# First adaLN part of a DiT layer kernel: k tiles in four column blocks of the TensorE array

## The chip, the cores and the metric

One core of a Trainium2 chip runs the whole layer in one launch. The metric is the device time of one execution in microseconds (us). The engines are named as in the profile: PE is TensorE (PEld its weight loads), DVE is VectorE, ACT is ScalarE, POOL is GpSimd, and SP issues the DMAs. Every engine takes its instructions strictly in the order of its own queue, and waits at the head of the queue until the semaphores of that instruction are there.

## The reference, cut to what matters

The layer works on 1024 latent tokens and 256 context tokens, both 1024 wide. The part that is changed is the adaLN modulation of the first normalisation:

```python
sh1, sc1, g1, sh2, sc2, g2 = ada_split(c, w_ada, b_ada)          # latents
csh1, csc1, ...            = ada_split(c_ctx, w_ada, b_ada)      # context
# ada_split: jnp.split(jax.nn.silu(cond) @ w_ada + b_ada, 6)
h   = LN(x)   * (1 + sc1)  + sh1
h_c = LN(ctx) * (1 + csc1) + csh1
p   = h @ W_in
```

So two vectors of 1024 values (SiLU of c and of c_ctx) are multiplied by the first 2048 columns of w_ada, 8 MB of float32. All of it is float32, and the kernel keeps that accuracy.

## The kernel before

The program begins with the first adaLN part, `ada1`. It runs over eight column groups j = 0 to 7. Group j gives shift and scale of 128 channels, that is 256 columns of w_ada, and its weights come in two DMAs of 512 KB (`wa{j}_0` with k tiles 0 to 3, `wa{j}_1` with k tiles 4 to 7) into a pool of seven buffers (`x_tile`, tag "x"), which the two context tiles `x_c0` and `x_c1` and later the latent tiles share. A DMA into a buffer waits until the last reader of what was in it is done, and no more than eight DMAs are under way, since their eight semaphores are used in turn.

`ada1_mm(j)` (L264) multiplies. The stationary operand is the pair of SiLU vectors for one k tile, padded with zeros to 128 columns; the moving operand is 128x256 of the weights. Five k tiles (L270) are plain float32 matmuls, each of which the profile shows as two MATMUL passes. The last three k tiles (ADA_SPLIT) go through `mm3` (L206 to L209): the weights are split into a rounded part `ahi` (ACT, L121) and the rest `alo` (DVE, L122), and three single-pass matmuls are made of them. All eight add up in one PSUM tile `pa_{j}`, of which two rows count. DVE copies these out as `arow_{j}` (L276).

`ada1_fin(j)` (L279) turns the two rows into columns with two small transposes (L282) into `pat_{j}`, and DVE adds the bias (L284, `mod`).

Between these stands the work on the context: statistics of the two context tiles (L178, L180), the POOL power (L171), the normalised tile `z_c0`, `z_c1` (L250), its transposes on PE (L188), shift and scale on ACT (L298, `hc`), and the split into `Hhi` (ACT, L305) and `Hlo` (DVE, L306), first for channels 0 to 511, after j = 3, and then for the rest. The 256 context tokens then go through the k columns of W_in (`kctx`, weights `hi_K`, `lo_K`), then both contexts and the eight latent chunks through the v and gate columns (`vg_8_0`, `vg_8_1`, `vg_9_0`, ... , weights `hi_VG`, `lo_VG`), with each latent chunk's own normalisation and split (`Hhi` L197, `Hlo` L198) in between, and the q weights (`hi_Q`, `lo_Q`) prepared beside them.

The kernel is written in a Tile framework that places the instructions of each engine in an order of its own, with a model of the times, when the program is built; that order is then fixed. Which instruction stands behind which on each engine is therefore not the order of the source lines.

Of the kernel before, what the change touches and what calls it, by code (L numbers as in the profile page):

```python
# [10 lines left out]
F32 = mybir.dt.float32  # L11
F32R = mybir.dt.float32r
AF = mybir.ActivationFunctionType
ALU = mybir.AluOpType
# [3 lines left out]
P = 128  # L18
# [4 lines left out]
KT = 8  # L23
# [7 lines left out]
BATCHES = (4, 3, 3, 3, 3)  # L31
USLOTS = (9, 29)
SLOT = 2112
ADA_SPLIT = 3


@with_exitstack
def layer_kernel(ctx: ExitStack, tc: tile.TileContext, I: dict, out: bass.AP, dbg=None):
    nc = tc.nc
    V, S, G, T = nc.vector, nc.scalar, nc.gpsimd, nc.tensor  # L40

    def dma(o, i):
        nc.sync.dma_start(o, i)
# [11 lines left out]
    wpool = wst.enter_context(tc.tile_pool(name="wpool", bufs=4))  # L55
# [19 lines left out]
    def ps_nm(name):  # L75
        return ps_next("nm", 5, 3, name)
# [19 lines left out]
    econ = early.enter_context(tc.tile_pool(name="econ", bufs=1))  # L96
# [3 lines left out]
    sp = st0.enter_context(tc.tile_pool(name="start", bufs=2, reuse_waits="tile"))  # L100

    def x_tile(name):
        return sp.tile([P, D], F32, tag="x", bufs=7, name=name)
# [4 lines left out]
    ada_w = []  # L108

    def ada1_load(j):  # L110
        rw = [x_tile(f"wa{j}_{i}") for i in range(2)]
        for i in range(2):
            dma(rw[i], I["wada1"][j, :, i * D : (i + 1) * D])
        hi = wpool.tile([P, SLOT], F32R, tag="whi", name=f"ahi_{j}").rearrange("p (k c) -> p k c", c=264)
        lo = wpool.tile([P, SLOT], F32R, tag="wlo", name=f"alo_{j}").rearrange("p (k c) -> p k c", c=264)
        rv = [t.rearrange("p (k c) -> p k c", c=256) for t in rw]
        for i in range(2):
            k0 = max(KT - ADA_SPLIT, 4 * i)
            if k0 < 4 * i + 4:
                src, ks = rv[i][:, k0 - 4 * i :, :], slice(k0, 4 * i + 4)  # L120
                S.copy(hi[:, ks, 0:256], src)  # L121
                V.tensor_tensor(lo[:, ks, 0:256], src, hi[:, ks, 0:256].bitcast(F32), ALU.subtract)  # L122
        ada_w.append((hi, lo, rv))

    ada1_load(0)
    cst = econ.tile([P, 576], F32, name="cst")
    dma(cst, I["consts"])
    ident = cst[:, 0:128]
    mask = [cst[:, 128:256], cst[:, 256:384]]
    lsel = cst[:, 384:512]  # L130
    onehot = cst[:, 512:576]
    bada1 = const.tile([P, KT, 2], F32, name="bada1")
    dma(bada1, I["bada1"])
    mhalf = const.tile([P, NH], F32, name="mhalf")
# [3 lines left out]
    zeros = econ.tile([P, P], F32, name="zeros")  # L138
# [3 lines left out]
    sc_s = const.tile([P, KT, 2], F32, name="silu_cc")  # L142
# [63 lines left out]
    def mm3(o, ahi, alo, bhi, blo, start, stop):  # L206
        T.matmul(o, ahi, blo, start=start, stop=False)  # L207
        T.matmul(o, ahi, bhi, start=False, stop=False)  # L208
        T.matmul(o, alo, bhi, start=False, stop=stop)  # L209
# [41 lines left out]
        return z  # L251


    shi = sp.tile([P, ADA_SPLIT, P], F32R, tag="shi", bufs=1, name="shi")
    slo = sp.tile([P, ADA_SPLIT, P], F32R, tag="slo", bufs=1, name="slo")
    s32 = sp.tile([P, KT - ADA_SPLIT, P], F32, tag="s32", bufs=1, name="s32")
    for t in (shi, slo, s32):
        V.tensor_copy(t, zeros.unsqueeze(1).broadcast_to(list(t.shape)))
    sc1 = sc_s[:, KT - ADA_SPLIT :, :]
    V.tensor_copy(s32[:, :, 0:2], sc_s[:, : KT - ADA_SPLIT, :])  # L260
    V.tensor_copy(shi[:, :, 0:2], sc1)
    V.tensor_tensor(slo[:, :, 0:2], sc1, shi[:, :, 0:2].bitcast(F32), ALU.subtract)

    def ada1_mm(j):  # L264
        hi, lo, rv = ada_w[j]
        pa = ps_nm(f"pa_{j}")
        n32 = KT - ADA_SPLIT
        for k in range(KT):
            if k < n32:
                T.matmul(pa[:, 0:256], s32[:, k, :], rv[k // 4][:, k % 4, :], start=(k == 0), stop=(k == KT - 1))  # L270
            else:
                mm3(
                    pa[:, 0:256], shi[:, k - n32, :], slo[:, k - n32, :], hi[:, k, 0:256], lo[:, k, 0:256], k == 0, k == KT - 1
                )
        ar = sp.tile([2, 256], F32, tag="arow", bufs=3, name=f"arow_{j}")
        V.tensor_copy(ar, pa[0:2, 0:256])  # L276
        return ar

    def ada1_fin(j, ar):  # L279
        pt = ps_nm(f"pat_{j}")  # L280
        for h in range(2):
            T.transpose(pt[:, 2 * h : 2 * h + 2], ar[:, h * P : (h + 1) * P], ident[0:2, 0:2])  # L282
        for h in range(2):
            V.tensor_scalar(mod1[:, j, h, :], pt[:, 2 * h : 2 * h + 2], bada1[:, j, h : h + 1], float(h), ALU.add, ALU.add)  # L284

    ctx_tok = NT - NCTX
    ada1_load(1)
    xc = []
    for c in range(NCTX):
        ada1_load(2 + c)  # L290
        xc.append(load_x(I["ctx"][c * P : (c + 1) * P, :], f"c{c}"))
# [19 lines left out]
    for j in range(KT):  # L311
        if 4 <= j + 3 < KT:
            ada1_load(j + 3)
        if j == 4:
            wK = prep_slot(I["win"][0], 2048, "K")
        ar = ada1_mm(j)
        if j == 3:
            zt = [
                h_transpose(zc[0], [ps_tr("zc0a"), ps_tr("zc0b")]),
                h_transpose(zc[1], [ps_mm(f"zc1{q}").rearrange("p (k t) -> p k t", k=4) for q in range(2)]),  # L320
            ]
        if prev is not None:
            ada1_fin(*prev)
            if prev[0] == 3:
                for q in range(4):
                    ctx_affine(q)
                ctx_split(0)
            if prev[0] > 3:
                ctx_affine(prev[0])
        prev = (j, ar)  # L330
# [9 lines left out]
    dma(bgate, I["bgate"].partition_broadcast(P))  # L340

    ada1_fin(*prev)
    ctx_affine(KT - 1)
    ctx_split(4)
# [955 lines left out]
    for i in range(2):  # L1300
        t, slot = ualloc(f"c11_{i}")
# [35 lines left out]
    f = hF[0]  # L1337
# [47 lines left out]
    for si in range(nx, len(steps)):  # L1385
        p, g, b = steps[si]
# [57 lines left out]
    for s2i in range(p2_done, len(steps2)):  # L1444
        p, c = steps2[s2i]
# [7 lines left out]
        if c == 7:  # L1453
# [9 lines left out]
            elif p == 3:  # L1463
                for t in range(4):
                    load_xt(t)
                for q in range(2):
                    x = ualloc(f"c12_{q}")
                    for h in range(2):
                        t = 2 * q + h
# [44 lines left out]


def _consts():
    c = np.zeros((P, 576), np.float32)
    c[:, 0:128] = np.eye(P, dtype=np.float32)
    s, t = np.arange(P)[:, None], np.arange(P)[None, :]
    c[:, 128:256] = np.where(s <= t, 0.0, NEG)  # L1520
    c[:, 256:384] = np.where(s >= t, 0.0, NEG)
    c[:, 384:512] = (s // 64) == (t // 64)
    for i in range(NCH):
        for h in range(NH):
            c[i * NH + h, 512 + i * NH + h] = 1.0
# [79 lines left out]
```

## Time and profile before

| | us |
|---|---|
| median of 3 runs | 1126.34 |
| lowest, highest | 1125.40, 1127.55 |
| the profiled execution | 1127.33 |
| its span, first to last instruction | 1125.4 |
| PE busy | 1094.6 (97%) |
| DVE, ACT, POOL busy | 761.5 (68%), 517.6 (46%), 53.6 (5%) |
| chain that ended last: PE, DVE, DMA | 89%, 4%, 3% |

The share of busy time is a mean over the whole program. The changed part lies in the first 44 us, so the views below are cut to that stretch and to the 60 us behind it: what each engine did in order of time (the timeline, which gives start, duration, engine, line, operation, tiles, and in brackets the idle time before and what ended it), the chain of waits, and the busy time by stretch. A matmul's end is modelled and overlaps the next one, so the time between starts, not the duration, is what one costs in a row of them.

### The profile page before, as it was taken

Reading aid. Unit: us, or ns where it says so; the run is one execution under the profiler, and the core shown is the slowest. Engines: PE = TensorE matmul, PEld = TensorE weight load, DVE = VectorE, ACT = ScalarE, POOL = GpSimd, SP = SyncE. Lnnn points to the kernel's source line nnn. Section 1 sums busy time; section 2 is a strip of 40 time slices with the busy share of each in tenths; the row PEclk is TensorE's granted clock in tenths of the full one; section 3 lists DMA queues with packets and bytes.
Section 4 is the critical chain, followed back from the end, with each engine's and each line's share of the span. In section 5 each row is a group of like instructions: output and inputs, shape, how many; then the busy total and the mean of one; then the engine's idle time right before and its main releaser. Section 6 shows DMA issues by size and latency. Waiting matters only on the chain.

```text
span 1125.4 us, 14624 instructions
## 1 busy us (share of the span) xinstructions
PE 1094.6 (97%) x5271; PEld 899.9 (80%) x5271; DVE 761.5 (68%) x1363; ACT 517.6 (46%) x821; POOL 53.6 (5%) x81
## 2 busy tenths in 40 slices
PE   8999999899999999997999999999999999999996
PEld 6899788777777888885888888888888888887875
DVE  4793666677775367659974747474667555468997
ACT  3585543321121236567755555556534334434341
POOL 0010000000101011110000000000000000001101
PEclk9999999999999999998999999999999999999999
DMA  8782579776453773233454435355997334356911
GB/s 319 259 280 95 169 255 293 236 204 175 127 155 113 260 238 129 85 112 112 151 195 127 175 123 183 112 197 201 321 413 271 113 90 152 96 168 235 326 57 75
DMA packets 92416, 208.08 MB, mean 185 GB/s; under 512 B 10037, under 2 KB 31413, under 8 KB 92089
## 3 DMA queue, kind: packets, MB, share of 16 engines
q1 hardware_dynamic: 92344, 207.16, 55.0%
q8 instruction: 41, 0.67, 0.2%
q14 instruction: 31, 0.25, 0.1%
HBM read 155.91 MB, written 51.21 MB: 184 GB/s over the span
## 4 chain that ended last, share of the span: by engine, by line
PE 89%; DVE 4%; DMA 3%; ACT 2%; issue 1%; POOL 1%; SPq 0%; DVEq 0%; ACTq 0%; POOLq 0%
PE A L986 29%; PE B L986 23%; PE wo L209 3%; PE wo L207 3%; PE wo L208 3%; PE n L736 2%; PE n L735 2%; PE pa L270 2%; PE v L207 2%; PE vg L209 1%; PE vg L208 1%; PE vg L207 1%; PE u L207 1%; PE v L209 1%; PE v L208 1%; PE u L209 1%
## 5 line engine op out<-in xcount | busy, mean ns | idle before, releaser
L986 PE MATMUL A<-wh,pb 128*128 128x512 f32 (+1 forms) x528 | 158.6, 383 | 0.0
L986 PE MATMUL B<-wh,pb 128*128 128x512 f32 x384 | 118.7, 390 | 0.0
L986 PEld LDWEIGHTS A<-wh,pb 128*128 128x128 f32 x528 | 98.0, 188 | 19.8
L986 PE MATMUL A<-wl,pb 128*128 128x512 f32 (+1 forms) x264 | 101.7, 385 | 3.2 <-DVE nmu_n L874 1.5
L986 PEld LDWEIGHTS B<-wh,pb 128*128 128x128 f32 x384 | 72.1, 188 | 15.6
L986 PE MATMUL B<-wl,pb 128*128 128x512 f32 x192 | 74.9, 390 | 0.0
L1206 ACT CAST pb<-a_S 128x1024 fp32r<-128x1024 f32 x32 | 33.7, 1053 | 75.1 <-PE B L986 43.8
L880 POOL TENSOR_TENSOR rs_n<-ve_n,mhalf 128x1 f32<-128x1 f32 x23 | 29.4, 1279 | 720.2 <-DVE ve_n L878 681.4
L1113 DVE TENSOR_TENSOR wc<-w1x,wc 128x512 fp32r<-128x512 f32 x56 | 38.3, 692 | 35.9 <-ACT wc L1112 35.9
L1207 DVE TENSOR_TENSOR wl<-b,wh 128x1024 fp32r<-128x1024 f32 x40 | 48.7, 1222 | 19.9 <-ACT wh L1206 6.9
L986 PEld LDWEIGHTS A<-wl,pb 128*128 128x128 f32 x264 | 49.6, 188 | 14.5 <-DVE nmu_n L874 1.7
L1207 DVE TENSOR_TENSOR pb<-a_S,pb 128x1024 fp32r<-128x1024 f32 x32 | 39.1, 1223 | 31.7 <-ACT pb L1206 31.5
L1206 ACT CAST wh<-b 128x1024 fp32r<-128x1024 f32 x40 | 42.0, 1051 | 33.4 <-DVE pb L1207 16.0
L207 PE MATMUL wo<-lo_W,yh 128*128 128x512 f32 x128 | 52.0, 406 | 0.0
L209 PE MATMUL wo<-hi_W,yl 128*128 128x512 f32 x128 | 50.7, 396 | 0.0
L208 PE MATMUL wo<-hi_W,yh 128*128 128x512 f32 x128 | 50.5, 394 | 0.0
L207 PE MATMUL vg<-lo_VG,Hhi 128*128 128x264 f32 x160 | 45.9, 287 | 0.0
L209 PE MATMUL vg<-hi_VG,Hlo 128*128 128x264 f32 x160 | 45.4, 284 | 0.5 <-DVE Hlo L198 0.5
L707 ACT ACTIVATE nmb<-nmb 128x512 f32<-128x512 f32 x16 | 10.1, 633 | 76.8 <-DVE nmb L706 46.6
L208 PE MATMUL vg<-hi_VG,Hhi 128*128 128x264 f32 x160 | 45.3, 284 | 0.0
L1112 ACT CAST wc<-w1x 128x512 fp32r<-128x512 f32 x56 | 34.4, 619 | 22.4 <-PE A L986 10.6
L1206 ACT CAST pb<-a_A 128x1024 fp32r<-128x1024 f32 x24 | 25.3, 1054 | 41.4 <-PE A L986 20.3
(412 smaller groups left out, 2773.7 us busy)
## 6 DMA issues: line engine op xcount, KB each, us to landing
ad<-in_wada SPq DMA_DIRECT2D x32, 512.0 KB, 6.1
b<-in_w SPq DMA_DIRECT2D x32, 512.0 KB, 5.2
a_S<-d_S SPq DMA_DIRECT2D x32, 512.0 KB, 4.1
d_S<-hF SPq DMA_DIRECT2D x50, 256.0 KB, 2.2
a_A<-d_A SPq DMA_DIRECT2D x24, 512.0 KB, 5.0
d_A<-hF SPq DMA_DIRECT2D x36, 256.0 KB, 2.0
wa<-in_wada SPq DMA_DIRECT2D x16, 512.0 KB, 6.2
w1x<-in_w SPq DMA_DIRECT2D x16, 512.0 KB, 3.6
```

Source lines behind the costliest of these rows:

```text
L207: T.matmul(o, ahi, blo, start=start, stop=False)
L208: T.matmul(o, ahi, bhi, start=False, stop=False)
L209: T.matmul(o, alo, bhi, start=False, stop=stop)
L270: T.matmul(pa[:, 0:256], s32[:, k, :], rv[k // 4][:, k % 4, :], start=(k == 0), stop=(k == KT - 1))
L735: T.matmul(pn[:, hh, :], nmb[d][:, h, :], vc[:, h, :], start=True, stop=False)
L736: T.matmul(pn[:, hh, :], wib[o : o + 64, h, :], st[o : o + 64, h, :], start=False, stop=True)
L880: G.tensor_tensor(rs, ve, mhalf[:, :1], op=ALU.pow)
L986: T.matmul(o, a, b, start=start and i == 0, stop=stop and i == 2, skip_group_check=more)
L1112: S.copy(t[:, 0:512], src)
L1113: V.tensor_tensor(t[:, 512:1024], src, t[:, 0:512].bitcast(F32), ALU.subtract)
L1206: S.copy(hi, src)
L1207: V.tensor_tensor(lo, src, hi.bitcast(F32), ALU.subtract)
```

## The change

All eight k tiles of a group become plain float32 matmuls, and the stationary operand shrinks from 128 columns to 32 (two that count and thirty zeros). K tile k goes to column block k modulo 4 of the array, and so to PSUM partitions 32q to 32q + 31 of `pa_{j}`; k tiles 4 to 7 add to what 0 to 3 left there. The split of the weights (ACT, DVE) and of the SiLU vectors goes. DVE now copies 128 partitions by 256 columns out as `arow_{j}`, and instead of the two transposes two float32 products with a 0/1 matrix `quads` (128x2) add the four partial sums and turn them at once.

```diff
-ADA_SPLIT = 3
@@ ada1_load
-        hi = wpool.tile([P, SLOT], F32R, tag="whi", name=f"ahi_{j}").rearrange(...)
-        lo = wpool.tile([P, SLOT], F32R, tag="wlo", name=f"alo_{j}").rearrange(...)
-        rv = [t.rearrange("p (k c) -> p k c", c=256) for t in rw]
-        for i in range(2):
...
-                S.copy(hi[:, ks, 0:256], src)
-                V.tensor_tensor(lo[:, ks, 0:256], src, hi[:, ks, 0:256].bitcast(F32), ALU.subtract)
-        ada_w.append((hi, lo, rv))
+        ada_w.append([t.rearrange("p (k c) -> p k c", c=256) for t in rw])
@@
-    shi = sp.tile([P, ADA_SPLIT, P], F32R, tag="shi", bufs=1, name="shi")
-    slo = sp.tile([P, ADA_SPLIT, P], F32R, tag="slo", bufs=1, name="slo")
-    s32 = sp.tile([P, KT - ADA_SPLIT, P], F32, tag="s32", bufs=1, name="s32")
...
+    s32 = sp.tile([P, KT, 32], F32, tag="s32", bufs=1, name="s32")
+    G.memset(s32, 0.0)
+    V.tensor_copy(s32[:, :, 0:2], sc_s)
@@ ada1_mm
         for k in range(KT):
-            if k < n32:
-                T.matmul(pa[:, 0:256], s32[:, k, :], rv[k // 4][:, k % 4, :], start=(k == 0), stop=(k == KT - 1))
-            else:
-                mm3(...)
-        ar = sp.tile([2, 256], F32, tag="arow", bufs=3, name=f"arow_{j}")
-        V.tensor_copy(ar, pa[0:2, 0:256])
+            q = k % 4
+            T.matmul(
+                pa[32 * q : 32 * q + 32, 0:256],
+                s32[:, k, :],
+                rv[k // 4][:, k % 4, :],
+                start=k < 4,
+                stop=k >= 4,
+                tile_position=(0, 32 * q),
+                skip_group_check=True,
+            )
+        ar = sp.tile([P, 256], F32, tag="arow", bufs=3, name=f"arow_{j}")
+        V.tensor_copy(ar, pa[:, 0:256])
@@ ada1_fin
-            T.transpose(pt[:, 2 * h : 2 * h + 2], ar[:, h * P : (h + 1) * P], ident[0:2, 0:2])
+            T.matmul(pt[:, 2 * h : 2 * h + 2], ar[:, h * P : (h + 1) * P], quads, start=True, stop=True)
```

With other instructions the framework sets another order, on all engines, up to about the second latent chunk; behind it the order is the old one. Three places show it. In the changed kernel the lines have other numbers: L255 is the matmul of L270, L271 the product that replaces the transposes of L282.

PE, groups 1 and 2 (`pa_1`, `pa_2`), before:

```order
L270 MATMUL pa_1_270<-wa1_0_193,s32_186 128x256 x4
L270 MATMUL pa_1_270<-wa1_1_194,s32_186 128x256
L282 MATMUL pat_0_287<-cst_95,arow_0_260 128x2 x2
L270 MATMUL pa_2_300<-wa2_0_201,s32_186 128x256
L207 MATMUL pa_1_270<-alo_1_198,shi_184 128x256
L208 MATMUL pa_1_270<-ahi_1_197,shi_184 128x256
L209 MATMUL pa_1_270<-ahi_1_197,slo_185 128x256
```

and in the changed kernel, from group 0 on:

```order
L255 MATMUL pa_0_223<-wa0_0_87,s32_180 32x256 x4
L255 MATMUL pa_0_223<-wa0_1_88,s32_180 32x256 x4
L271 MATMUL pat_0_249<-cst_91,arow_0_232 128x2 x2
L255 MATMUL pa_1_238<-wa1_0_183,s32_180 32x256 x4
L255 MATMUL pa_1_238<-wa1_1_184,s32_180 32x256 x4
L271 MATMUL pat_1_269<-cst_91,arow_1_247 128x2 x2
L255 MATMUL pa_2_258<-wa2_0_187,s32_180 32x256 x4
L255 MATMUL pa_2_258<-wa2_1_188,s32_180 32x256 x4
L271 MATMUL pat_2_309<-cst_91,arow_2_267 128x2 x2
L255 MATMUL pa_3_278<-wa3_0_193,s32_180 32x256 x4
L179 MATMUL zc0a_289<-cst_91,z_c0_208 128x128 x4
```

The finishing of group 0 stood behind five matmuls of group 1; now each group's finishing stands right behind its own matmuls and ahead of those of the next group.

DVE, around the two normalised context tiles, before:

```order
L250 TENSOR_SCALAR z_c0_230<-x_c0_209,mv_c0_224,rs_c0_228 128x1024
L122 TENSOR_TENSOR alo_3_216<-wa3_1_212,ahi_3_215 128x3x256
L178 BN_STATS st_c1_232<-x_c1_219 128x6 x2
L284 TENSOR_SCALAR mod1_109<-pat_2_367,bada1_97 128x2
L180 BN_AGGR mv_c1_235<-st_c1_232 128x2
L276 COPY arow_3_345<-pa_3_330 2x256
L169 TENSOR_SCALAR ve_c1_237<-mv_c1_235 128x1
L284 TENSOR_SCALAR mod1_109<-pat_2_367,bada1_97 128x2
L250 TENSOR_SCALAR z_c1_241<-x_c1_219,mv_c1_235,rs_c1_239 128x1024
```

and in the changed kernel:

```order
L241 TENSOR_SCALAR z_c0_208<-x_c0_191,mv_c0_202,rs_c0_206 128x1024
L265 COPY arow_3_287<-pa_3_278 128x256
L273 TENSOR_SCALAR mod1_105<-pat_3_339,bada1_93 128x2 x2
L169 BN_STATS st_c1_210<-x_c1_197 128x6 x2
L295 TENSOR_TENSOR Hlo_104<-hc0_221,Hhi_103 128x4x128
L171 BN_AGGR mv_c1_213<-st_c1_210 128x2
L160 TENSOR_SCALAR ve_c1_215<-mv_c1_213 128x1
L241 TENSOR_SCALAR z_c1_219<-x_c1_197,mv_c1_213,rs_c1_217 128x1024
```

The copy and finishing of group 3 and the `Hlo` of the first context tile now stand ahead of `z_c1`, which had nothing of group 3's finishing in front of it.

ACT, around the first latent chunk (`h32_l0`, `Hhi`) and the q weights, before:

```order
L195 ACTIVATE h32_l0_693<-pt_l0_1_684,mod1_109 128x128 x4
L358 COPY va_9_704<-vg_9_0_706 128x2x128
L197 CAST Hhi_107<-h32_l0_693 128x8x128
L358 COPY va_9_704<-vg_9_1_734 128x2x128
L89 CAST hi_Q_797<-raw_Q_0_799 128x1024
```

and in the changed kernel:

```order
L347 COPY va_9_618<-vg_9_0_620 128x2x128
L186 ACTIVATE h32_l0_607<-pt_l0_0_597,mod1_105 128x128 x4
L186 ACTIVATE h32_l0_607<-pt_l0_1_598,mod1_105 128x128 x4
L88 CAST hi_Q_711<-raw_Q_0_713 128x1024
L188 CAST Hhi_103<-h32_l0_607 128x8x128
```

The cast of the q weights, which has to wait for their DMA, moved from behind the first latent chunk's `Hhi` to ahead of it. SP issues that DMA (`raw_Q_0`) now behind the store of the first v chunk (`d_va`), where it stood ahead of it before.

## Rows read from the trace of the kernel before

**Rows 1.** A stretch: PE, PEld, DVE, ACT, POOL busy (instructions), clock, DMA share, GB/s.

```profile
15.00:20.00 5.00, 5.00 (x31) 4.29 (x30) 3.63 (x10) 0.84 (x1) 0.55 (x1) 1.00 1.03 407
```

**Rows 2.** The chain of waits in 0 to 110 us: start, us, what.

```profile
4.86 4.61 PE pa L270 x10
...
11.18 2.16 PE pa L270 x10
...
38.71 0.25 DVE arow L276
...
43.21 0.70 DVE Hlo L306
43.95 0.38 PE kctx L207
```

**Rows 3.** Timeline of PE, groups 2 and 3 and the context transposes.

```profile
17.32 0.28 PE L208 MATMUL pa<-ahi,shi 128*128 128x256 f32 x1
...
17.44 0.28 PE L209 MATMUL pa<-ahi,slo 128*128 128x256 f32 x1
...
21.57 0.28 PE L282 MATMUL pat<-cst,arow 2*128 2x2 f32 x2
...
25.16 1.09 PE L188 MATMUL zc<-cst,z_c 128*128 128x128 f32 x8 [0.32 <-DVE z_c L250]
```

**Rows 4.** Timeline of PE much later: small float32 products, 128 columns stationary.

```profile
163.30 1.84 PE L420 MATMUL pad<-ones,adacc 128*128 128x1 f32 x16
```

**Rows 5.** Timeline of DVE, POOL and ACT, 16 to 44 us.

```profile
16.48 1.26 DVE L178 BATCH_NORM_STATS2 st_c<-x_c 128x6 f32<-128x512 f32 x2
...
18.47 0.41 DVE L276 COPY arow<-pa 2x256 f32<-2x256 f32 x1 [0.48 <-PE pa L209]
...
19.09 0.55 POOL L171 TENSOR_TENSOR rs_c<-ve_c,mhalf 128x1 f32<-128x1 f32 x1 [17.50 <-DVE mod L284]
...
19.68 0.81 DVE L250 TENSOR_SCALAR z_c<-x_c,mv_c,rs_c 128x1024 f32<-128x1024 f32 x1 [0.61 <-POOL rs_c L171]
...
24.29 0.81 DVE L250 TENSOR_SCALAR z_c<-x_c,mv_c,rs_c 128x1024 f32<-128x1024 f32 x1 [0.54 <-POOL rs_c L171]
...
25.86 1.16 ACT L298 ACTIVATE hc<-zc,mod 128x128 f32<-128x128 f32 x3 [0.89 <-PE zc L188]
...
26.94 0.35 DVE L284 TENSOR_SCALAR mod<-pat,bada 128x2 f32<-128x2 f32 x2 [0.96 <-PE pat L282]
...
28.03 0.62 ACT L305 CAST Hhi<-hc 128x512 fp32r<-128x512 f32 x1
...
28.98 0.67 DVE L306 TENSOR_TENSOR Hlo<-hc,Hhi 128x512 fp32r<-128x512 f32 x1
...
36.03 2.00 ACT L89 CAST hi_K<-raw_K 128x1024 fp32r<-128x1024 f32 x2
...
39.18 1.20 DVE L90 TENSOR_TENSOR lo_K<-raw_K,hi_K 128x1024 fp32r<-128x1024 f32 x1
```

**Rows 6.** DMA issues by tile: KB each, us from issue to landing; and SP's timeline.

```profile
raw_Q<-in_win SPq DMA_DIRECT2D x2, 512.0 KB, 4.6
...
52.05 0.38 SPq L43 DMA_DIRECT2D raw_Q<-in_win  x1
```

**Rows 7.** Timeline of ACT and PE, v weights and first latent chunk.

```profile
46.73 1.06 ACT L89 CAST hi_VG<-raw_VG 128x1056 fp32r<-128x1056 f32 x1
...
58.86 1.11 ACT L197 CAST Hhi<-h_l 128x1024 fp32r<-128x1024 f32 x1
...
60.08 1.11 ACT L89 CAST hi_Q<-raw_Q 128x1024 fp32r<-128x1024 f32 x1
...
61.52 0.39 PE L209 MATMUL vg<-hi_VG,Hlo 128*128 128x264 f32 x1 [0.53 <-DVE Hlo L198]
```

**Rows 8.** Stretches around a wait of PE at 202 us; columns as in rows 1.

```profile
201.92:205.34 3.42, 1.23 (x11) 1.02 (x10) 3.42 (x5) 0.27 (x1) 0.00 (x0) 1.00 0.70 252
205.34:208.75 3.41, 3.41 (x11) 2.65 (x10) 2.36 (x6) 2.65 (x6) 0.00 (x0) 0.50 0.94 277
```

More of the change, by code (lines that the diff above doesn't have):

```diff
@@ L113, in ada1_load @@
             dma(rw[i], I["wada1"][j, :, i * D : (i + 1) * D])
-        hi = wpool.tile([P, SLOT], F32R, tag="whi", name=f"ahi_{j}").rearrange("p (k c) -> p k c", c=264)
-        lo = wpool.tile([P, SLOT], F32R, tag="wlo", name=f"alo_{j}").rearrange("p (k c) -> p k c", c=264)
-        rv = [t.rearrange("p (k c) -> p k c", c=256) for t in rw]
-        for i in range(2):
-            k0 = max(KT - ADA_SPLIT, 4 * i)
-            if k0 < 4 * i + 4:
-                src, ks = rv[i][:, k0 - 4 * i :, :], slice(k0, 4 * i + 4)
-                S.copy(hi[:, ks, 0:256], src)
-                V.tensor_tensor(lo[:, ks, 0:256], src, hi[:, ks, 0:256].bitcast(F32), ALU.subtract)
-        ada_w.append((hi, lo, rv))
+        ada_w.append([t.rearrange("p (k c) -> p k c", c=256) for t in rw])
     ada1_load(0)
-    cst = econ.tile([P, 576], F32, name="cst")
+    cst = econ.tile([P, 578], F32, name="cst")
     dma(cst, I["consts"])
@@ L131, in layer_kernel @@
     onehot = cst[:, 512:576]
+    quads = cst[:, 576:578]
     bada1 = const.tile([P, KT, 2], F32, name="bada1")
@@ L251, in norm_x @@
         return z
-    shi = sp.tile([P, ADA_SPLIT, P], F32R, tag="shi", bufs=1, name="shi")
-    slo = sp.tile([P, ADA_SPLIT, P], F32R, tag="slo", bufs=1, name="slo")
-    s32 = sp.tile([P, KT - ADA_SPLIT, P], F32, tag="s32", bufs=1, name="s32")
[L257 to L262, printed above, removed]
+    s32 = sp.tile([P, KT, 32], F32, tag="s32", bufs=1, name="s32")
+    G.memset(s32, 0.0)
+    V.tensor_copy(s32[:, :, 0:2], sc_s)
     def ada1_mm(j):
-        hi, lo, rv = ada_w[j]
+        rv = ada_w[j]
         pa = ps_nm(f"pa_{j}")
-        n32 = KT - ADA_SPLIT
         for k in range(KT):
-            if k < n32:
-                T.matmul(pa[:, 0:256], s32[:, k, :], rv[k // 4][:, k % 4, :], start=(k == 0), stop=(k == KT - 1))
-            else:
-                mm3(
-                    pa[:, 0:256], shi[:, k - n32, :], slo[:, k - n32, :], hi[:, k, 0:256], lo[:, k, 0:256], k == 0, k == KT - 1
-                )
-        ar = sp.tile([2, 256], F32, tag="arow", bufs=3, name=f"arow_{j}")
-        V.tensor_copy(ar, pa[0:2, 0:256])
+            q = k % 4
[10 more added lines that the diff above has]
+        V.tensor_copy(ar, pa[:, 0:256])
         return ar
@@ L1516, in _consts @@
 def _consts():
-    c = np.zeros((P, 576), np.float32)
+    c = np.zeros((P, 578), np.float32)
     c[:, 0:128] = np.eye(P, dtype=np.float32)
@@ L1522, in _consts @@
     c[:, 384:512] = (s // 64) == (t // 64)
+    c[:, 576:578] = s % 32 == np.arange(2)
     for i in range(NCH):
```

## The prediction

> **What bounds the kernel now.** Look at the stretch view first. In the middle of the changed part PE is busy all of the time, at the full granted clock, while the DMA engines are loaded to 1.03 of their time at 407 GB/s [rows 1]. So two things are near their limit at once, and a faster PE soon meets the loads. Then the chain of waits: it runs through the PE matmuls of `pa` from 4.86 us on, leaves PE at 38.71 with the copy of the last group, and passes through bias, shift, `Hhi` and `Hlo` until PE takes up the context's k columns again at 43.95 [rows 2]. Behind that PE has work without a gap until it waits 0.53 us for the first latent chunk's `Hlo` at 61.5 [rows 7]. A microsecond gained or lost up to there comes out at the end of the program, because what follows keeps its order and is bound by PE (97% of the whole span). So the question is when PE gets through that point, and the terms are made against it. The profiled execution took 1127.33 us, 1 us over the median of the three; the sum is made on the former and 1 us is taken off at the end.
>
> **The change part by part.** One float32 pass of 256 columns costs 0.216 us (ten in 2.16), and 0.46 in the first ten, before 10.8 us, at what must be half the clock [rows 2]. A float32 k tile is two passes, 0.43. A pass of the split kind costs 0.12 from start to start, and the two transposes 0.2 [rows 3]. One group is now 10 x 0.216 + 9 x 0.12 + 0.2 = 3.4 us of PE, eight of them 27.6.
>
> The new group has 16 float32 passes. How far the column blocks run beside each other no row tells, since no matmul of before is put into a column block. The bounds are one after the other, 16 x 0.216 = 3.46, and all four abreast, 4 x 0.216 = 0.86. I take a middle: the two passes of one block use the same columns and must follow each other, and the engine starts matmuls in order, so the second pass of block q can run beside the first of block q + 1, but no more: 9 x 0.216 = 1.94.
>
> Now the wait that comes with it. The finishing of a group stands right behind its own matmuls on PE, and the next group's matmuls are queued behind it. So PE stands still in each group from its last matmul until the copy is there: 0.16 for the matmul's end (0.28 long, 0.12 apart [rows 3]), 0.41 for the copy [rows 5] and some 0.08 for two semaphores, 0.65. Before, five matmuls of the next group covered this. The copy of 128 partitions has the same 256 columns, so I keep 0.41. The selector products are float32 with 128 columns stationary; sixteen such passes took 1.84 us, 0.115 each [rows 4], so four of them are 0.46, against 0.2 for the transposes. A group is then 1.94 + 0.65 + 0.46 = 3.05 us: only 0.4 less than before, of 1.5 that the matmuls give. The eight ACT casts and DVE subtractions that go lay beside PE and the loads; I give nothing for them. The zero fill on POOL and the new columns of the constants lie before the first weights land; nothing.
>
> There is a rule of the Trainium skill that speaks against the change here, on the page "TensorEngine Tiling (Array Packing)", section "Key Properties": going from one tiling mode to another drains the array. The kernel does so twice in each group, but no row here shows it, and it is in no term.
>
> Next the chain to `z_c0` and `z_c1`. At half clock group 0 ends its matmuls at 4.86 + 9 x 0.43 = 8.7, its finishing at about 10.3; group 1 then runs to 12.3, group 2 from 13.4 to 15.35, and its bias is done at 15.35 + 0.65 + 0.46 + 0.1 + 0.35 = 16.9. Behind it on DVE stand the statistics (1.26, then 0.3), the POOL power 0.65 with its hand-over, and `z_c0` 0.81 [rows 5]: 20.0, half a us earlier than now (20.49). PE has meanwhile done the first half of group 3 and waits 2.5 us. Then transposes 0.6, the other half of group 3 1.1, copy 0.65, products 0.46, bias 0.45: 23.3. The statistics of the second context tile end at 24.6, but the first tile's `Hlo` now stands ahead of the rest, and waits for four shifts on ACT (1.5, three took 1.16) and `Hhi` 0.62; it ends at 23.3 + 1.5 + 0.6 + 0.7 = 26.1. Then 0.3, the power 0.65 and 0.81: `z_c1` is done at 27.9, where it was at 25.1 [rows 5]. PE has waited since about 24.0 and still has 8 transposes 0.9 (the row of 1.09 [rows 3] less its tail), the rest of group 4 0.65, groups 5 to 7 with 3 x 1.94, and four finishings (0.46 each) of which two waits of 0.65 are not covered: 27.9 + 0.9 + 0.65 + 5.8 + 3 x 0.46 + 1.3 = 37.9; the last copy follows, where it began at 38.71. So 0.6 us is left of the gain.
>
> Then the tail. Copy, products and bias end at 37.9 + 0.65 + 0.46 + 0.5 = 39.5. On ACT two shifts (0.8), the second cast of the k weights (1.0) and two `Hhi` (1.2) follow; on DVE the two subtractions for the k weights (1.2 each) stand ahead of `Hlo`, and the second ends at 39.5 + 0.8 + 1.0 + 1.2 = 42.5; two `Hlo` of 0.65 make it 43.8 [rows 5]. PE takes up k at 43.8 against 43.95: nothing gained.
>
> Behind it: three of the four casts of the v weights (1.06 each [rows 7]) now stand behind the copies of `kctx`, and PE has to wait for the last parts, 0.3 to 0.8 us; I take 0.5. And the q weights: their DMA is issued behind the store of the first v chunk, which is done some 10.7 us after PE takes up k, at 54.5; with 4.6 to land [rows 6] it is 59.5 to 60.5 (the row of before was issued at 52.05). Its cast 1.1 and then the latent `Hhi` 1.1 [rows 7] end at 62.2, `lo_Q` and `Hlo` on DVE after that at 64; PE is out of work at about 61 (43.8 + 3.0 + 13.4 as before + 0.5). It waits about 2.5 us where it waited 0.5, so 2.0. Sum so far: 2.4 us slower, with bounds of 0.5 and 4.
>
> Last the clock. At 202 us PE worked 1.23 of 3.42 us, and in the 3.41 us that followed the granted clock was 0.50, that is the lower of its two levels, 1.2 GHz [rows 8]: 1.7 us lost, if PE is the bound there. PE now waits 2.5 us for `z_c0` and 3.9 for `z_c1`, and what comes next is on the path. Bounds are none and two such stretches, 0 to 3.4, more if the clock also rises later at the start; I take 3. Together 5.5: 1127.3 + 5.5 - 1 = 1132 us, and by the bounds of these terms 1127 to 1134, or 1136 with a later rise at the start.
>
> **The rivals.** First, the four blocks run fully abreast. Then a group is 0.86 + 0.65 + 0.46 = 1.97 us, less than its loads need (1 MB at 407 GB/s, 2.6 us), and the loads set the pace: `z_c1` is done near 25.5 and the last group near 33.5. K weights land where they did, so PE takes up k near 39, 5 us earlier; the waits for v (0.5 to 1) and for q (2 to 3) stay, as those hang on the orders. That leaves 1 to 3 us: 1125 us, with 1123 to 1127 if the clock holds, and up to 1131 where the still lower load on PE takes it down. It decides if eight k tiles take under 1.1 us. For it speaks that the blocks write to different partitions and share nothing. This is the case that the Trainium skill, page "TensorE: Matmul & The Clock Gate", Part 3, describes: matmuls of different column blocks start some 4 ns apart, and three blocks gave 2.38 times the speed. The same part says that matmuls start and end in program order, which is what holds two-pass float32 back to the middle; no row here shows either. Chance 26%.
>
> Second, the blocks do not overlap, and the change does not do what it says: 3.46 + 1.11 = 4.57 us a group, 1.2 more than now. All eight groups are then on the path: 8 x 1.2 = 9.3. The later `z_c1`, the waits for v and q and the clock come on top as above, 3 to 7, so 12 to 16: 1140 us. Against it speaks only that the stationary operand is in other columns. Chance 19%.
>
> Third, the clock stays at the lower level throughout, since PE waits in each group. The passes and products (2.40 us of a group) then cost twice: 19 us for eight groups, less the first, which is at that level now (2.4), and less the two waits (6.4), which shrink; some 10 us over the 2.4: 1139 us. For it: the full clock came only after 6 us of PE without a gap [rows 2]. Against: PE is still busy four fifths of a group, 2.40 of 3.05 us. Chance 12%.
>
> **How the numbers follow.** The forecast has 43%: 39 slower by over 0.2% (2.25 us, about what a measurement of this kernel can tell from no change) and 4 within. Of the first rival's 26, 12 are faster, 9 within, 5 slower. The other two (19 and 12) are slower. So faster 12%, same 13%, slower 75%. The range takes in the first rival from 1124.5 and most of the second, up to 1142; its own range is 1127 to 1136.
>
> **What would show it.** In the trace after: starts of two neighbouring passes of `pa` 0.216 apart with nine to a group (the middle), 0.05 (abreast) or sixteen to a group (none); PE idle of about 0.6 before each `pat`, put down to `arow`; `z_c1` ending at 27 to 30 rather than 25; PE back at `kctx` near 44; a wait of 2 us or more before the first latent v chunk, behind `hi_Q`; a granted clock of 0.50 after 17 or after 24 us. The forecast is wrong if the matmuls of a group take under 1.1 us, or if PE comes to the first latent chunk before 60 us.

## The result and the profile after

The changed kernel takes 1135.05 us, median of five runs (1133.38 to 1139.38); the kernel before took 1126.34 in five runs beside it. The ratio is 1.0079, with a 95% interval of 1.0061 to 1.0098: slower, 3 us above the predicted 1132. The profiled execution has a span of 1133.8 us, the one of before 1125.4, so 8.4 us are to be found in it. The time came out near the forecast, but not for the reasons of the forecast.

First the stretches of the changed kernel, in the columns of [rows 1]. The clock column reads 1.00 until the profile records a first change of the clock, here at 50.6 us; which level held before that has to be read from how long a pass takes.

```profile
15.00:20.00 5.00, 2.47 (x20) 1.13 (x12) 2.57 (x8) 0.00 (x0) 0.55 (x1) 1.00 1.03 410
...
25.00:30.00 5.00, 2.75 (x16) 1.52 (x9) 3.07 (x7) 1.09 (x3) 0.55 (x1) 1.00 0.51 175
...
45.00:50.00 5.00, 5.00 (x25) 5.00 (x25) 3.60 (x4) 2.17 (x4) 0.00 (x0) 1.00 0.79 238
...
66.50:70.00 3.50, 0.93 (x6) 0.54 (x4) 3.12 (x6) 3.44 (x7) 0.55 (x1) 1.00 0.72 286
71.10:74.50 3.40, 3.40 (x18) 3.40 (x17) 3.40 (x5) 2.40 (x4) 0.10 (x1) 0.50 0.94 271
```

In 15 to 20 us, where PE was busy all the time before [rows 1], it now works 2.47 of 5 us. In 45 to 50 us it is busy throughout, with 25 matmuls, where it ran 44 before. The timeline of PE tells the pass times:

```profile
13.52 1.93 PE L255 MATMUL pa<-wa,s 128*32 128x256 f32 x16
16.00 1.01 PE L271 MATMUL pat<-cst,arow 128*128 128x2 f32 x4 [0.55 <-DVE arow L265]
...
50.08 0.41 PE L200 MATMUL kctx<-Hhi,lo_K 128*128 128x256 f32 x1
...
50.68 0.28 PE L200 MATMUL kctx<-Hhi,lo_K 128*128 128x256 f32 x1
...
68.60 0.39 PE L198 MATMUL vg<-lo_VG,Hhi 128*128 128x264 f32 x1 [1.91 <-ACT Hhi L188]
...
70.05 0.39 PE L200 MATMUL vg<-hi_VG,Hlo 128*128 128x264 f32 x1 [0.71 <-DVE Hlo L189]
```

In the first line a whole group, 16 passes, takes 1.93 us. They start in fours: 13.517, 13.524, 13.530, 13.537, then 13.945 and so on, 0.43 apart. So the four blocks run fully abreast, and each pass takes twice the 0.216 of [rows 2]: PE is at the lower of its two levels, 1.2 GHz. It stays there through all eight groups and nearly all of `kctx`, whose matmuls start 0.21 apart up to 50.5 us and 0.12 from then on. Before, a pass takes 0.216 us from 11.18 us on [rows 2], and the first recorded clock, 1.00, is at 10.8.

The chain of waits between 0 and 80 us shows what set the pace (start, us, what):

```profile
27.96 0.82 DVE z_c L241
28.83 1.97 PE zc L179 x8
...
39.59 1.91 PE pa L255 x16
41.52 0.43 DVE arow L265
42.00 1.02 PE pat L271 x4
...
60.54 5.99 DMA raw_Q<-in_win
66.56 1.05 ACT hi_Q L88
67.63 1.22 DVE lo_Q L89
68.85 1.15 DVE Hlo L189
```

And the waits of PE in the first 45 us, in total, how often, and the longest:

```profile
PE pa L255 <- DMA wa<-in_wada: 6.1, 4, 4.9
PE pat L271 <- DVE arow L265: 3.3, 6, 0.5
PE zc0a L179 <- DVE z_c L241: 2.6, 1, 2.6
PE zc L179 <- DVE z_c L241: 2.3, 1, 2.3
```

The account of the 8.4 us: the k columns of the context end at 52.5 us, where they ended at 46.9, 5.6 us later. Some 3 of these are the lower level in `kctx` itself: from 44.6, when the k weights are complete, to 50.5 it takes 5.9 us for what the full clock does in half. The rest is that the last group's matmuls end at 41.5 (38.7 before [rows 2]), so less of k is done ahead of that. At the first latent chunk PE waits 1.91 + 0.71 us, where it waited 0.53 [rows 7]: 2.1 us more. Behind that wait the clock is at 0.50 for 3.4 us while PE is busy all the time: about 1.7 us. These are 9.4 us. At 86 us of the kernel before, the same matmuls come 10.3 us later in the changed one; where the other 0.9 arise is not worked out. 1.3 us come back near 205 us, where the kernel before has a stretch at 0.50 [rows 8] and the changed one has none, and at the end the difference is the 8.4 us.

### The profile page after: what moved, and what is told of

Read it like the earlier page. It is cut to its first block, busy times and chain, and to the rows that moved or that the text cites. A ratio compares the mean times of both kernels' runs of the same rounds, so it can differ in the third digit from the quotient of the medians.

```text
span 1133.8 us, 14571 instructions
## 1 busy us (share of the span) xinstructions
PE 1093.7 (96%) x5263; PEld 889.6 (78%) x5263; DVE 754.1 (67%) x1350; ACT 510.4 (45%) x813; POOL 54.6 (5%) x82
## 4 chain that ended last, share of the span: by engine, by line
PE 87%; DVE 5%; DMA 4%; ACT 2%; issue 1%; POOL 0%; SPq 0%; DVEq 0%; ACTq 0%; POOLq 0%
PE A L975 29%; PE B L975 23%; PE wo L200 3%; PE wo L198 3%; PE wo L199 3%; PE n L725 2%; PE n L724 2%; PE v L198 2%; DMA ad<-in_wada 2%; PE u L198 2%; PE v L200 1%; PE vg L200 1%; PE v L199 1%; PE u L200 1%; PE u L199 1%; PE vg L199 1%
## 5 line engine op out<-in xcount | busy, mean ns | idle before, releaser
L1102 DVE TENSOR_TENSOR wc<-w1x,wc 128x512 fp32r<-128x512 f32 x56 | 38.2, 689 | 35.9 <-ACT wc L1101 35.9
L200 PE MATMUL wo<-hi_W,yl 128*128 128x512 f32 x128 | 50.6, 395 | 0.0
L199 PE MATMUL wo<-hi_W,yh 128*128 128x512 f32 x128 | 50.5, 394 | 0.0
L696 ACT ACTIVATE nmb<-nmb 128x512 f32<-128x512 f32 x16 | 10.1, 631 | 76.4 <-DVE nmb L695 42.6
L1101 ACT CAST wc<-w1x 128x512 fp32r<-128x512 f32 x56 | 34.4, 618 | 22.2 <-PE A L975 10.7
```

The lines of the kernel that those rows point to most:

```text
L696: S.activation(w, w, AF.Exp)
L1101: S.copy(t[:, 0:512], src)
L1102: V.tensor_tensor(t[:, 512:1024], src, t[:, 0:512].bitcast(F32), ALU.subtract)
```

## The experiments

My theory after reading this: the blocks give all of what the first rival said, but the faster a group is done, the more PE waits, for the copy, for the loads, for `z_c`; and with these waits the clock doesn't come up. The rivals: the orders of the q and v weights alone; the uncovered copy alone; and that the clock isn't tied to PE's waits.

Several kernels need the order on PE to stand still. In them each PE instruction of the adaLN part is queued behind the one before (`last`) by hand. A fill is a float32 product of two constant 128x128 tiles into a spare bank that nobody reads. The other engines keep the order that the framework gives them, and with another PE program that can move too. Each trace is one execution of its kernel.

### The base, and fills in PE's waits

`e0_pinned`:

```diff
+    def behind():
+        return tc.issue_after(last.ins) if last is not None else ExitStack()
...
-            T.matmul(
+            with behind():
+                last = T.matmul(
```

> The changed kernel with the order on PE written out by hand as it stands in the trace of the changed kernel (transposes of a context tile behind the first half of groups 3 and 4, each finishing behind its own matmuls); the only other move is that the first context tile's Hlo stands behind z_c1 on DVE. It is the base for the fills. Clock theory (the loss is PE at its lower clock level up to 50 us): the clock still comes only near 50 us, time 1133 to 1136. Order theory (the loss is the order of the q and v weights): the same 1133 to 1136. If the Hlo ahead of z_c1 were the cause: 0.7 us or more faster than the changed kernel.

1134.41 us against 1124.51 of before, ratio 1.0084 (1.0069 to 1.0099): the base behaves as the changed kernel. `z_c1` ends 0.4 us earlier, at 28.4, without the first tile's `Hlo` ahead of it, and nothing comes of it.

`e1_fill` (the fills are 54; the 50 of the expectation is a miscount, and it doesn't name the two between the halves of groups 0 and 1):

```diff
+    def fill(n):
+        nonlocal last
+        for _ in range(n):
+            with behind():
+                last = T.matmul(fbank[:, 0:P], zeros, ones, start=True, stop=True)
+
+    fill(8)
+    MID, TAIL = (2, 2, 2, 2, 2, 2, 2, 2), (3, 3, 2, 0, 0, 0, 0, 0)
...
             if k == 3 and j in (3, 4):
+                fill(10 if j == 3 else 10)
...
+            elif k == 3 and j in (0, 1):
+                fill(1)
+        fill(MID[j])
...
+        fill(TAIL[j])
```

`fill(8)` stands ahead of group 0, `MID` behind a group's matmuls, `TAIL` behind its finishing, and the ten ahead of a context tile's transposes.

> As e0_pinned, with 50 float32 products of 128 columns that nothing reads put into PE's waits of the adaLN part: eight ahead of group 0, two behind each group's matmuls, two or three behind the first three finishings, ten ahead of the transposes of each context tile. Nothing is left out. Clock theory: passes of pa 0.216 us apart from about 10 us on instead of 0.43 up to 50 us; PE is through kctx near 44 us (52.6 in the changed kernel), part of it is lost again at the q weights: 1124 to 1129. Order theory: PE comes earlier to the latent chunk but waits there for hi_Q, 1133 to 1136. Copy theory (the wait of 0.55 us for the copy in each group is the loss): no change, 1133 to 1136, as the fills stand in the wait and the wait stays.

1124.93 us against 1124.51, ratio 1.0003 (0.9991 to 1.0014): the whole loss is gone, by work that nobody needs. The timeline of PE in `e1_fill`:

```profile
13.25 1.07 PE L272 MATMUL pa<-wa,s 128*32 128x256 f32 x16
14.25 0.71 PE L260 MATMUL fill<-ones,zeros 128*128 128x128 f32 x4
14.87 0.61 PE L299 MATMUL pat<-cst,arow 128*128 128x2 f32 x4
...
34.13 0.39 PE L198 MATMUL kctx<-Hlo,hi_K 128*128 128x256 f32 x1
...
57.80 0.39 PE L198 MATMUL vg<-lo_VG,Hhi 128*128 128x264 f32 x1 [1.97 <-ACT Hhi L188]
```

Sixteen passes in 1.07 us: four rounds of 0.216 and the end of the last. The fills stand exactly in the wait for the copy, so that wait is as long as it was; the copy theory falls. PE begins k at 34.1 instead of 42.9, and the wait behind the q weights is still there at 57.8.

Not only the fills differ. On DVE the statistics of the second context tile stand behind group 3's copy and first bias in `e0_pinned`, and ahead of that copy in `e1_fill`. DVE in `e0_pinned`, and then in `e1_fill`:

```profile
23.53 0.42 DVE L277 COPY arow<-pa 128x256 f32<-128x256 f32 x1 [3.10 <-PE pa L262]
...
25.20 1.28 DVE L169 BATCH_NORM_STATS2 st_c<-x_c 128x6 f32<-128x512 f32 x2
...
27.58 0.81 DVE L241 TENSOR_SCALAR z_c<-x_c,mv_c,rs_c 128x1024 f32<-128x1024 f32 x1 [0.67 <-POOL rs_c L162]
```

```profile
19.74 1.29 DVE L169 BATCH_NORM_STATS2 st_c<-x_c 128x6 f32<-128x512 f32 x2 [0.70 <-DMA x_c<-in_ctx]
20.95 0.41 DVE L291 COPY arow<-pa 128x256 f32<-128x256 f32 x1
...
22.32 0.81 DVE L241 TENSOR_SCALAR z_c<-x_c,mv_c,rs_c 128x1024 f32<-128x1024 f32 x1
```

So `z_c1` is done 8.0 us behind `z_c0` in the one and 4.1 behind it in the other. How much of the 9.5 us between the two kernels is due to that can be estimated. In `e6_fill_no_z`, which has the order of `e0_pinned`, `z_c1` is done 4.4 us after the start of group 3's copy. That copy could start at 20.8 in `e1_fill`, so with the old order `z_c1` would be done near 25.3, half a us after the transposes begin there (24.85, behind the ten fills). `e4_pairs` below has the moved order without a fill, and its ratio is still 1.0059. Most of the gain is then the fills' own.

`e5_fill_start` has only the eight ahead of group 0:

```diff
-                fill(10 if j == 3 else 10)
...
-                fill(1)
...
+    MID, TAIL = (0, 0, 0, 0, 0, 0, 0, 0), (0, 0, 0, 0, 0, 0, 0, 0)
```

> e0_pinned with the eight fills ahead of group 0 alone (PE busy from 1.2 us on), none in the waits. Clock theory in its narrow form (the waits in and between the groups keep the clock down, not the late start): passes stay 0.43 apart up to 50 us, 1133 to 1136. If only the missing work before 4.9 us kept the clock down: full clock by 10 us, 1125 to 1128.

1132.14 us against 1125.20, ratio 1.0063 (1.0048 to 1.0078). Timeline of PE, and two stretches in the columns of [rows 1]:

```profile
6.26 0.64 PE L272 MATMUL pa<-wa,s 128*32 128x256 f32 x8 [0.80 <-DMA wa<-in_wada]
...
9.38 1.08 PE L272 MATMUL pa<-wa,s 128*32 128x256 f32 x8 [1.33 <-DMA wa<-in_wada]
```

```profile
4.80:8.90 4.10, 1.89 (x20) 0.86 (x20) 0.77 (x3) 0.00 (x0) 0.00 (x0) 0.88 1.03 320
8.90:12.30 3.40, 2.18 (x17) 0.42 (x17) 0.42 (x1) 0.00 (x0) 0.00 (x0) 0.50 1.03 420
```

The clock is up when group 0 starts, so a late start isn't the cause. PE works 1.89 of the next 4.1 us, the clock falls at 7.9, and the second group runs at 0.50 again. That half of the narrow clock theory holds: an early full clock doesn't outlast the first groups with their waits. The other half, slow passes up to 50 us, does not: full passes come back for groups 5 to 7, and `kctx` is slow once more up to 45.4 us. Yet from 10.7 us on PE does the same work with the same waits as in `e0_pinned`, every start 0.15 us earlier, up to these two lines, `e0_pinned` first:

```profile
31.97 1.02 PE L285 MATMUL pat<-cst,arow 128*128 128x2 f32 x4 [0.55 <-DVE arow L277]
```

```profile
31.81 0.61 PE L295 MATMUL pat<-cst,arow 128*128 128x2 f32 x4 [0.55 <-DVE arow L287]
```

In `e5_fill_start` the full clock begins there, in `e0_pinned` at 50.2 us. So PE's work and waits of these 21 us do not settle when the clock comes back, and the 2.4 us by which the ratio of `e5_fill_start` is lower are not clear of the two intervals.

`e6_fill_no_z` is `e1_fill` without one line:

```diff
-                fill(10 if j == 3 else 10)
```

> e1_fill without the ten fills ahead of each context tile's transposes: PE waits some 2.5 us for z_c0 and as long for z_c1. If such a wait alone takes the clock down, as the prediction had it, 0.43 us passes come back after 17 or 24 us and stay for some time: 1126 to 1133. If the clock holds: 1123 to 1125, at or below e1_fill, whose ten fills ahead of z_c1 ended 1.7 us after z_c1.

1133.40 us (1128.96 to 1135.63) against 1125.20, ratio 1.0061 (1.0038 to 1.0085); it spreads more than the others. PE's timeline and stretches:

```profile
16.35 0.64 PE L272 MATMUL pa<-wa,s 128*32 128x256 f32 x8
19.49 1.97 PE L179 MATMUL zc<-cst,z_c 128*128 128x128 f32 x8 [2.50 <-DVE z_c L241]
...
27.04 1.97 PE L179 MATMUL zc<-cst,z_c 128*128 128x128 f32 x8 [2.85 <-DVE z_c L241]
```

```profile
31.00:42.60 11.60, 11.60 (x77) 7.73 (x77) 2.91 (x10) 3.35 (x7) 0.00 (x0) 0.50 0.50 177
```

This is the mechanism that the prediction named, a fall after each of the two waits for `z_c` (the transposes behind them take 1.97 instead of 1.09; the clock is 0.50 from 19.1 to 22.5 and again from 25.9). What the prediction had wrong is how long it lasts: from 25.9 to 49.8 us, and that although PE shows no gap at all in 31.0 to 42.6. Two limits: the trace is of the slowest of the four runs, and DVE's order is that of `e0_pinned` again, so `z_c1` comes 7.6 us behind `z_c0` and the second wait is longer than the missing fills alone would make it.

`b0_before_fill` puts the eight into the kernel before:

```diff
+    for _ in range(8):
+        with tc.issue_after(last.ins) if last is not None else ExitStack():
+            last = T.matmul(fbank[:, 0:P], zeros, ones, start=True, stop=True)
```

> The kernel before with eight fills ahead of group 0. It tells whether an earlier full clock is worth as much without the change. In the kernel before the clock rises at 10.8 us by itself; with the fills by 8 us or earlier. PE saves up to 3 us in group 0 and 1, of which the loads and the chain to z_c0 may take back all: 1122 to 1126. If the gain of e1_fill were one of fills as such and not of the clock lost by the change, it would be 9 us here too.

1125.39 us against 1125.20, ratio 1.0004 (0.9994 to 1.0013): no difference, though the first recorded full clock is at 7.3 us instead of 10.8. An earlier full clock is worth nothing there; the 9.5 us between `e0_pinned` and `e1_fill` belong to the change.

### The blocks themselves

`e4_pairs` asks why the blocks run abreast: it issues the two k tiles of a block one behind the other.

```diff
-        for k in range(KT):
+        for k in (0, 4, 1, 5, 2, 6, 3, 7):
...
-            if k == 3 and j in (3, 4):
+            if k == 5 and j in (3, 4):
```

> e0_pinned with the eight k tiles of a group in the order 0, 4, 1, 5, 2, 6, 3, 7, so that the two of one column block follow each other directly; same instructions, same order on the other engines. If the blocks run abreast only because neighbours in the program are in different blocks (starts in program order), a group takes about 13 passes instead of 4 and 1139 to 1146 us if the clock stays low, less if the busier PE raises the clock. If each block has a queue of its own, a group stays at 4 passes where both loads are there, and the time at that of e0_pinned (1134).

1131.67 us against 1125.20, ratio 1.0059 (1.0044 to 1.0074). PE's timeline:

```profile
4.91 1.03 PE L262 MATMUL pa<-wa,s 128*32 128x256 f32 x2 [4.91 <-DMA wa<-in_wada]
6.27 1.95 PE L262 MATMUL pa<-wa,s 128*32 128x256 f32 x14 [0.34 <-DMA wa<-in_wada]
...
14.45 1.95 PE L262 MATMUL pa<-wa,s 128*32 128x256 f32 x16
...
31.00 1.09 PE L262 MATMUL pa<-wa,s 128*32 128x256 f32 x16
```

A group still takes four rounds (1.95 at the lower level, 1.09 at the full one), not 13. So k tile 1 starts beside k tile 4 although it is issued behind it, and k tile 2 before k tile 5 has started. That doesn't hang on the modelled ends: DVE's copy of the group that starts at 14.45 begins at 16.52. A block works off its own matmuls and doesn't hold the others back; that PE takes its instructions strictly in the order of its queue, as the section on the cores has it, isn't so for matmuls of different blocks. Only a wait holds back all: in the first line one matmul runs, the next one waits for the second load, and k tile 1, whose load is there, runs only after it. By the ratios the time is some 2.8 us below `e0_pinned`, and the passes are at the full level from 26 us on for some 14 us. What brought that isn't parted here. The half of a group that stands ahead of a wait now takes four rounds instead of two, and PE waits less (in 15 to 20 us it works 4.27 of 5 us, against 2.33 in `e0_pinned`). And the other engines did not keep their order: DVE has that of `e1_fill`, and PE waits 0.18 us for `z_c1` instead of 2.41.

`e10_one_block` does the change without the blocks: all k tiles in float32, in one block.

```diff
-                    pa[32 * q : 32 * q + 32, 0:256],
+                    pa[0:32, 0:256],
...
-                    start=k < 4,
-                    stop=k >= 4,
-                    tile_position=(0, 32 * q),
+                    start=k == 0,
+                    stop=k == KT - 1,
+                    tile_position=(0, 0),
```

> e0_pinned with all eight k tiles of a group in the first column block (32 rows of the result, summed in place; copy and selector products take 32 rows). The plan of the other engines moves with it (the finishing of the last two groups goes in between k products, the q weights load earlier). The passes must follow each other: 16 to a group. Clock theory: PE is busier, the clock rises early as in the kernel before, a pass is 0.216 us, a group 3.46 us of passes against 1.93 at half clock: 1132 to 1140, that is no more than some us over the four blocks although PE has four times the passes in a row. If blocks at the lower clock were not the cause of the loss, one block would cost 8 x 1.5 us over e0_pinned or more: 1144 and up.

1131.68 us against 1125.70, ratio 1.0065 (1.0047 to 1.0083). PE's timeline:

```profile
4.80 5.52 PE L261 MATMUL pa<-wa,s 128*32 128x256 f32 x16 [4.80 <-DMA wa<-in_wada]
...
11.35 3.64 PE L261 MATMUL pa<-wa,s 128*32 128x256 f32 x16
15.50 0.60 PE L284 MATMUL pat<-cst,arow 32*128 32x2 f32 x4 [0.50 <-DVE arow L276]
```

One block needs 16 rounds where four need 4, and the kernel isn't slower than the same with four: by the ratios it is 2.1 us faster, which the two intervals don't tell from nothing. The first group takes the clock up (its passes are 0.43 apart until 8.6 us and 0.216 after), and it stays up, with a wait of 0.50 us for the copy in each group. A part of this is the plan, which moved with the edit, so the size isn't the clock's alone. But a group of 3.64 us without fills loses nothing against one of 1.93.

### The orders

`e2_q_late` moves one line, the load and split of the q weights, behind the second latent chunk.

```diff
-    wQ = prep_slot(I["win"][1], 2048, "Q")
...
         vg_chunk(c, c)
+        if c == 1:
+            wQ = prep_slot(I["win"][1], 2048, "Q")
```

> The changed kernel with the load and split of the q weights written two chunks later (behind the second latent v chunk), so that no cast or subtraction of them stands ahead of the first latent tile's Hhi and Hlo. Order theory: PE's wait at 66 to 69 us goes (PE was busy 7.3 of 10 us there), and with it the stretch at half clock at 71 us: 1130 to 1132 if that is all of what the orders cost, 1127 if the whole loss lies there. Clock theory: what was lost before 53 us stays, 1130 or more; PE through kctx at 52.6 as before.

1131.80 us against 1124.51, ratio 1.0062 (1.0047 to 1.0077), 1.9 us below the changed kernel by the ratios, whose intervals overlap; the trace shows where it comes from. PE waits 0.21 and 0.72 at the latent chunk:

```profile
65.64 0.39 PE L198 MATMUL vg<-lo_VG,Hhi 128*128 128x264 f32 x1 [0.21 <-ACT Hhi L188]
67.12 0.39 PE L200 MATMUL vg<-hi_VG,Hlo 128*128 128x264 f32 x1 [0.72 <-DVE Hlo L189]
```

1.7 us of wait are gone, and the clock stays up behind it. The order of the q weights carries some 2 of the 9 us.

`b1_before_q_late` is the same edit in the kernel before.

> The kernel before with the q weights loaded and split two chunks later, the edit of e2_q_late. PE's and ACT's order stay as they are there; PE waited 0.53 us for the first latent chunk's Hlo. If the late q weights help only where the change moved them ahead, 1124.5 to 1126.5, within 0.2% of before; if they are worth 2 us by themselves, 1123 to 1124.

1125.57 us against 1125.70, ratio 1.0000 (0.9990 to 1.0010). The place of the q weights costs only where the change put it.

`e3_fill_q_late` has both edits, that of `e1_fill` and that of `e2_q_late`.

> Both: the fills of e1_fill and the late q weights of e2_q_late. If clock and order each carry a part of the loss, the gains add: 1119 to 1125, faster than the kernel before. If only one of them does, the time is that of e1_fill or of e2_q_late.

1123.29 us against 1124.51, ratio 0.9985 (0.9976 to 0.9994): the gains add. `e1_fill`'s 1.0003 less the 0.0017 of `e2_q_late` would be 0.9986. This although the clock was at 0.50 from 35.9 to 39.3 us in the trace, which it was not in `e1_fill` after the same PE work.

### A version that beats both

`e7_fill_short` is `e3_fill_q_late` with a shorter fill ahead of the second context tile's transposes:

```diff
-                fill(10 if j == 3 else 10)
+                fill(10 if j == 3 else 4)
```

> e3_fill_q_late with four fills instead of ten ahead of the second context tile's transposes, since the ten ended 1.7 us after z_c1 was there. Clock theory: the clock holds and PE is 1.4 us earlier at the last group, of which the K weights (landed at 32.3 us) let most pass: 1121 to 1122.5. If the shorter fill lets the clock fall behind z_c1, as in e6_fill_no_z: 1126 or more.

1120.64 us against 1125.86, ratio 0.9956 (0.9944 to 0.9968): faster than the kernel before by 5 us, and than the changed one by 1.2%. The transposes come at 24.07, and in 35 to 40 us, where the trace of `e3_fill_q_late` has its slow stretch, PE is at the full level; how much of the gain over `e3_fill_q_late` is each of the two is not shown:

```profile
24.07 1.04 PE L179 MATMUL zc<-cst,z_c 128*128 128x128 f32 x8
...
34.86 0.38 PE L200 MATMUL kctx<-Hhi,lo_K 128*128 128x256 f32 x1 [0.77 <-DVE lo_K L89]
```

`e9_cover` replaces the fills behind groups 4 to 6 by work: the next group's matmuls stand ahead of a group's finishing.

```diff
-    MID, TAIL = (2, 2, 2, 2, 2, 2, 2, 2), (3, 3, 2, 0, 0, 0, 0, 0)
+    MID, TAIL = (2, 2, 2, 2, 0, 0, 0, 2), (3, 3, 2, 0, 0, 0, 0, 0)
...
-        if prev is not None:
+        if prev is not None and prev[0] < 4:
             ada1_fin(*prev)
...
         ar = ada1_mm(j)
+        if prev is not None and prev[0] > 3:
+            ada1_fin(*prev)
+            ctx_affine(prev[0])
```

> e7_fill_short with work in place of fills: from group 4 on the next group's matmuls stand ahead of a group's finishing on PE and cover the wait for its copy, and the fills behind groups 4 to 6 go; the casts of the K weights thereby come ahead of the last shifts on ACT. Clock theory: the clock holds, k begins near 33.5 us instead of 35.5 and is through near 40: 1118 to 1121. If column-blocked matmuls without the full-array fills between them do not hold the clock: 1124 to 1129. If the loads (the last wada1 tile landed at 29.7, K weights at 32.3) bound it already: 1121 to 1123, as e7_fill_short.

1123.31 us against 1125.86, ratio 0.9975 (0.9966 to 0.9984): better than before, worse than with fills. The expected third case came with the second on top:

```profile
29.85 0.64 PE L272 MATMUL pa<-wa,s 128*32 128x256 f32 x8 [0.73 <-DMA wa<-in_wada]
...
33.34 0.58 PE L198 MATMUL kctx<-Hlo,hi_K 128*128 128x256 f32 x1 [1.42 <-ACT hi_K L88]
```

```profile
34.40:38.00 3.60, 3.56 (x17) 3.40 (x17) 3.33 (x5) 2.89 (x6) 0.00 (x0) 0.50 0.70 224
```

PE is done with the groups sooner, so it waits for the last tile of `wada1` and then 1.42 us for the k weights, and falls to the lower level for the first half of `kctx`. It looks like the change itself in small.

## Why the prediction was right, and where its steps failed

**The overlap of the blocks: the step that failed first.** It said that the second pass of a block can run beside the first of the next block and no more, nine passes to a group. It is four: 1.07 us at the full level in `e1_fill`, where the prediction itself said that it is wrong below 1.1. The first rival had this right, and its 1125 us for a clock that holds is near the 1124.93 of `e1_fill`. The Trainium skill, page "TensorE: Matmul & The Clock Gate", Part 3, has the blocks abreast, and there this case's trace agrees (starts 7 ns apart where it says some 4). The same part of the Trainium skill says that matmuls start in program order, and that had held my value back; `e4_pairs` shows the blocks starting past one another, so here the measurement decides. That a group took 1.93 us, where 1.94 had been predicted, is chance: four rounds at half the clock instead of nine at the full one.

**The clock: the term that was mis-sized.** The prediction gave it 3 us, for two stretches behind the waits for `z_c`, with a bound of 3.4 and "more" for a later rise. The fall behind these waits is there (`e6_fill_no_z`), but the lower level held from the start to 50.6 us and through `kctx`, where no wait stands. The fills that take it away give 9.5 us, some half a us of which is DVE's moved order by the estimate above. The third rival had the clock right and the overlap wrong; against it the prediction argued that PE would be busy four fifths of a group. From the first group to the k columns it was busy 28.6 of 38.0 us, three quarters, but in each of the last two groups 2.87 of 3.42, more than four fifths, and their passes were slow all the same. So the argument itself doesn't hold. The case that came, blocks abreast and the clock down, stood only in half a sentence of the first rival ("up to 1131 where the still lower load on PE takes it down").

**The copy and the products.** The wait was 0.55 us, in six of the eight groups, against 0.65 predicted. The four products take 0.53 us from start to start at the full level against 0.46. Both were right, and the copy wait matters by what it does to the clock, not by its length.

**The chain to `z_c`.** `z_c0` ended at 20.56 us and `z_c1` at 28.77, predicted 20.0 and 27.9. The order on DVE that stood behind this was right. Before, `z_c1` was done 4.6 us behind `z_c0`, now it is 8.2; no run changes that order alone, so its share of the loss stays open. `e4_pairs`, where it moved, is 2.8 us below `e0_pinned`.

**The tail.** PE came to the k columns at 42.9 and had all it needed at 44.6, predicted 43.8. The v weights cost PE nothing, against 0.5. The q weights cost 2.1 us, against 2.0, by the path that was named: the DMA behind the store of the first v chunk, the cast ahead of the latent `Hhi`; `e2_q_late` takes it away. Two slips of the text change nothing: it names four finishings behind `z_c1` and adds three, which is right, and 54.5 + 4.6 for the landing is 59.1.

So the sum came out 3 us low. The overlap was put too slow by 1.1 us a group, the clock too fast for 40 us, and the two errors met.

## What to carry to other kernels

When a matmul stage is made faster than what feeds it, PE gets waits, and the clock may go with them: then every pass doubles, in the stage and in the one behind it. Read the time of one pass, not only the busy share or the clock column, which says nothing until its first recorded change. Before giving up such a change, fill the waits with idle products, and look whether the plan of the other engines moved with them: if the loss goes and the plan stood, it was the clock, and the fills may stay in. And compare times of several runs, since two traces of the same work can have different clocks.

## What the hardware showed that was not expected

A busy PE alone does not bring the clock back. In `e6_fill_no_z` PE was busy 11.60 of 11.60 us between 31.0 and 42.6 with column blocks, fills and products, and stayed at 0.50; with the same work and ten products more ahead of each `zc`, `e1_fill` had the full level there. What tells the two apart no run here shows. Nor is the clock the same after the same work: in `e5_fill_start` it came back at 31.8 us and in `e0_pinned` at 50.2 with the same starts on PE for 21 us, and in `e3_fill_q_late` it fell at 35.9 us where it held in `e1_fill`.

Column blocks work off their matmuls independently, float32 with its two passes too, and in an order that isn't that of the program (`e4_pairs`). A wait of one matmul still holds back all that is issued behind it.

Going between the full array and four column blocks costs 0.1 us at the most, read from the starts of single matmuls. In `e1_fill` the first fill starts 0.31 us after the last pass of a group, and in the kernel before, where all is the full array, the first transpose starts 0.31 us after a pass of the same length. The way back takes 0.21 us, where fills are 0.11 apart. The drain that the Trainium skill, page "TensorEngine Tiling (Array Packing)", section "Key Properties", names for such a change of mode can't be more than that here.
